# Context scores in the banks of transposes and outputs, and weight parts of four output projection tiles in the normalised input's memory

## The chip, the core and the metric

The kernel runs on one NeuronCore of a Trainium2 chip. The core has TensorE (matmuls, written to eight PSUM banks), VectorE, ScalarE and GpSimd for elementwise work, and SyncE, which here only issues transfers. Each engine works through its own list of instructions in order, and semaphores hold an instruction until its inputs are there and its output memory is free. The metric is the time of one execution on the device in microseconds (us); less is better.

## What is computed

One step of a two-layer backbone on 640 tokens of width 1024: 128 context tokens and 512 latent tokens. Each layer normalises its input, projects it to the inputs of three mixers (differential attention, a state-space mixer, neighbourhood attention), merges their outputs through sigmoid gates and adds an output projection. What matters here:

```python
def _diff_attention(q, k, v, lam):          # 4 heads, two score maps (m) per head
    p = _softmax32(jnp.einsum('bqhmd,bkhmd->bhmqk', qb, k) * scale)
    p = p[:, :, 0] - lam * p[:, :, 1]
    return jnp.einsum('bhqk,bkhe->bqhe', p.astype(v.dtype), v)
...
# context tokens read the 128 context keys; latent tokens read 512 latent keys and 256 cached ones
...
    merged = (ma * ((ya * jax.nn.silu(ga)) @ w_br_a) + mb * (yb @ w_br_b)
              + mc * ((yc * jax.nn.silu(gc)) @ w_br_c))
    return x + gate * (merged @ w_out)
```

## The kernel before

Activations lie with channels on the partitions, so a projection is a chain of matmuls over eight blocks of 128 channels (`feat`, L175: 128 outputs by 320 tokens at a time, a "half" of the 640). Every product of two float32 factors is done as three matmuls of a high and a low part (`hi`, `lo`). A weight tile is loaded to `raw` (two buffers), ScalarE copies its high part (L150) and VectorE subtracts it for the low part (L151); the pools `whi` and `wlo` have three buffers each. `mm` has three PSUM banks.

PSUM in the differential attention: three banks `mm`, one tile `s` of three banks (pool `ps`, one buffer) for scores, one bank `t` for transposes and one bank `o` for outputs (pool `pp`, one buffer each).

`diff_attn` does one head: the context first, then four query tiles of 128 tokens. For a query tile TensorE writes both score maps to `s` (L547, L551), VectorE takes the row maxima of both (L510) and scales them (L511), ScalarE makes both exponentials with their sums (L513; the tiles `e0` and `e1` have one buffer each), VectorE combines the maps (L514, L515, L517). Then two sets of three transposes go through the one bank `t` (L558), each copied by ScalarE (`ph`, L560) and subtracted by VectorE (`pl`, L561), and after two query tiles 18 matmuls with the values (L566) and a copy (L568). The context is the same with 128 keys: scores L526, transpose L529, copy L531, product L533. `diff_norm` squares the output (L576), sums columns on TensorE (L201) and makes rows of factors (L593); `diff_out` applies them (L604). Other work is written around it and fills TensorE meanwhile: the value projections of the next heads (L187, split by ScalarE L422 and VectorE L423), projections for the next mixer, and merge gates (`logit`: tanh evacuation L1061).

`out_proj` runs once per half (tokens 0 to 319, then 320 to 639): eight tiles m of 128 output channels, each with its own weight tile; VectorE adds gate times result to x (L1110). Half 0 comes right after the last merges. The normalised input `h` (eight high and eight low tiles of 128 x 640) is not read any more by then.

The order of each engine's instructions is not that of the program text: an automatic scheduler orders the whole program by its own estimate of when each operation can start, within what buffers allow. A small edit can so move instructions far from it.

Of the kernel before, what the change touches and what calls it, by code (L numbers as in the profile page):

```python
# [36 lines left out]
LC = ((0,), (1,), (2, 3), (4, 5, 6, 7))  # L37
MA = ((0,), (), (1,), (2, 3))

M_ID, M_TF, M_TB, M_LE, M_GE, M_ONE = range(6)  # L40
# [82 lines left out]


class Net:
    def __init__(self, nc, tc, a, o, dump=None):
# [15 lines left out]
    def weights(self, src, k, n):  # L142

        nc = self.nc
        view = lambda t: t[:, 0:k * n].rearrange("p (k n) -> p k n", k=k)
        raw = view(self.wraw.tile([128, 1056], F32, tag="raw", name="raw"))
        self.dma(raw, src)
        hi = view(self.whi.tile([128, 1056], F32R, tag="hi", name="hi"))
        lo = view(self.wlo.tile([128, 1056], F32R, tag="lo", name="lo"))
        nc.scalar.activation(hi, raw, AF.Copy)  # L150
        nc.vector.tensor_tensor(out=lo, in0=raw, in1=hi, op=ALU.subtract)  # L151
        return hi, lo

    def w_part(self, l, m, part):
# [341 lines left out]
    def diff_attn(self, l, h, v, kq, nlam, p, cp, ps, pp, after_ctx):  # L496
# [9 lines left out]
        def soft(s, n, t):  # L506

            st = p.tile([128, 4], F32, tag="st", name="st", bufs=3)
            e = [p.tile([128, 768], F32, tag=f"e{m}", name="e", bufs=1)[:, 0:n] for m in range(2)]
            nc.vector.tensor_reduce(out=st[:, 0:2], in_=s, axis=AX.X, op=ALU.max)  # L510
            nc.vector.tensor_scalar(out=st[:, 0:2], in0=st[:, 0:2], scalar1=-0.125, scalar2=None, op0=ALU.mult)  # L511
            for m in range(2):
                nc.scalar.activation(e[m], s[:, m], AF.Exp, bias=st[:, m:m + 1], scale=0.125, accum_out=zz[:, t, m:m + 1])  # L513
            nc.vector.reciprocal(st[:, 2:3], zz[:, t, 1:2])  # L514
# [5 lines left out]
        def bank3():  # L520
            return ps.tile([128, 1536], F32, tag="s", name="s")


        s = bank3().rearrange("p (b n) -> p b n", b=3)[:, 0:2, 0:128]
        for m in range(2):
            nc.tensor.matmul(s[:, m, :], lhsT=qx[half[m], :], rhs=kx[half[m], :], start=True, stop=True)  # L526
        e = soft(s, 128, 0)
# [575 lines left out]

    def out_proj(self, l, mg, x, gate, half):
        nc, a = self.nc, self.a
        for m in range(8):
            def evac(_, ps):
# [4 lines left out]

            self.feat(self.weights(a["w_out"][l, m], 8, 128), mg, evac, halves=(half,))

# [174 lines left out]
```

## Time and profile before

| | |
|---|---|
| runs | 1611.29 us median of 3 (1610.94 to 1612.96) |
| profiled execution | 1611.84 us, span 1610.1 us |
| granted TensorE clock, mean | 0.997 |
| TensorE busy | 1583.1 us, 98% of the span |
| VectorE / ScalarE / GpSimd busy | 66% / 48% / 10% |

Times in a trace count from the start of the span; the 1.7 us between the span and the execution's time lie around it. TensorE is nearly always busy, so its idle stretches are what another order can win or lose. A wait is read as: idle time of the engine before an instruction, and who released it.

### The profile page before, as it was taken

How to read it: one execution, taken by the hardware profiler on the slowest of the kernel's cores; microseconds unless marked ns; L12 is line 12 of the kernel's file. 1: busy time of each engine (PE TensorE's matmuls, PEld its weight loads, DVE VectorE, ACT ScalarE, POOL GpSimd, SP SyncE). 2: the span in 40 equal slices, each digit the busy share in tenths (PEclk: the TensorE clock that was granted, in tenths of full speed). 3: DMA queues.
4: the chain of work that ended last, by engine and by line, in shares of the span. 5: the costliest groups of instructions: out<-in, count | busy, mean ns of one | idle time of the engine just before them, and what ended most of it. 6: DMA issues, size and time to landing. Idle time of an engine off the chain costs nothing.

```text
span 1610.1 us, 29172 instructions
## 1 busy us (share of the span) xinstructions
PE 1583.1 (98%) x11371; PEld 1508.3 (94%) x11371; DVE 1064.1 (66%) x2299; ACT 774.1 (48%) x1790; POOL 155.8 (10%) x182
## 2 busy tenths in 40 slices
PE   8999999999999999999999999999999999999998
PEld 5999899999999999999989989999999999999998
DVE  5865688667556566756677667676575575577565
ACT  4535654344445555443455466334444555454342
POOL 2003421011000000000000252101010000000000
PEclk9999999999999999999999999999999999999999
DMA  9663225321225343436543222452122543344543
GB/s 340 210 244 112 89 93 160 125 75 56 85 88 162 127 127 110 151 115 245 185 164 133 85 75 82 139 174 74 60 89 78 161 127 89 112 133 155 207 168 131
DMA packets 81673, 214.63 MB, mean 133 GB/s; under 512 B 9728, under 2 KB 25664, under 8 KB 80512
## 3 DMA queue, kind: packets, MB, share of 16 engines
q1 hardware_dynamic: 80624, 211.46, 40.1%
q8 instruction: 90, 1.47, 0.4%
q0 software_dynamic: 480, 0.88, 0.2%
q10 hardware_dynamic: 432, 0.43, 0.1%
q14 instruction: 47, 0.39, 0.1%
HBM read 170.27 MB, written 34.08 MB: 127 GB/s over the span
## 4 chain that ended last, share of the span: by engine, by line
PE 89%; DVE 4%; DMA 3%; ACT 1%; issue 1%; POOL 1%; SPq 0%; DVEq 0%; ACTq 0%; POOLq 0%
PE mm L175 61%; PE mm L187 7%; PE s L1001 2%; PE o L1025 2%; PE o L566 2%; PE t L1017 2%; PE ex L175 2%; PE s L551 1%; PE g L813 1%; PE t L558 1%; DMA aw<-in_w_ada 1%; PE y L826 1%; PE y L268 1%; PE s L547 1%; DMA qd<-qr 1%
## 5 line engine op out<-in xcount | busy, mean ns | idle before, releaser
L175 PE MATMUL mm<-hl,hi 128*128 128x320 f32 x1856 | 577.8, 311 | 0.8 <-DVE hl L383 0.8
L175 PE MATMUL mm<-hh,hi 128*128 128x320 f32 x1856 | 574.5, 310 | 3.3 <-ACT hh L382 2.8
L175 PE MATMUL mm<-hh,lo 128*128 128x320 f32 x1856 | 573.5, 309 | 0.2 <-DVE lo L151 0.2
L175 PEld LDWEIGHTS mm<-hh,hi 128*128 128x128 f32 x1856 | 348.4, 188 | 11.6 <-ACT hh L382 4.1
L175 PEld LDWEIGHTS mm<-hh,lo 128*128 128x128 f32 x1856 | 348.9, 188 | 7.3 <-issue 4.7
L175 PEld LDWEIGHTS mm<-hl,hi 128*128 128x128 f32 x1856 | 348.5, 188 | 6.3 <-issue 2.6
L151 DVE TENSOR_TENSOR lo<-raw,hi 128x1024 fp32r<-128x1024 f32 (+2 forms) x194 | 235.6, 1215 | 93.7 <-ACT hi L150 90.7
L150 ACT ACTIVATE hi<-raw 128x1024 fp32r<-128x1024 f32 (+2 forms) x194 | 200.1, 1032 | 177.5 <-PE mm L175 116.5
L175 PE MATMUL mm<-yh,hi 128*128 128x320 f32 x320 | 98.8, 311 | 1.1 <-DVE th L1080 0.7
L175 PE MATMUL mm<-yl,hi 128*128 128x320 f32 x320 | 99.0, 310 | 0.0
L175 PE MATMUL mm<-yh,lo 128*128 128x320 f32 x320 | 99.0, 310 | 0.0
L187 PE MATMUL mm<-hi,hh 128*128 128x264 f32 (+1 forms) x320 | 90.5, 284 | 1.8 <-DVE vl L423 1.7
L187 PE MATMUL mm<-lo,hh 128*128 128x264 f32 (+1 forms) x320 | 91.0, 285 | 0.0
L187 PE MATMUL mm<-hi,hl 128*128 128x264 f32 (+1 forms) x320 | 90.6, 284 | 0.0
L560 ACT ACTIVATE ph<-t 128x384 fp32r<-128x384 f32 x64 | 31.4, 490 | 113.9 <-PE t L558 113.9
L175 PE MATMUL mm<-mgh,hi 128*128 128x320 f32 x256 | 78.7, 311 | 1.7 <-ACT hi L150 1.7
L175 PE MATMUL mm<-mgl,hi 128*128 128x320 f32 x256 | 79.9, 312 | 0.0
L175 PE MATMUL mm<-mgh,lo 128*128 128x320 f32 x256 | 78.7, 309 | 1.0 <-DVE lo L151 1.0
L510 DVE TENSOR_REDUCE st<-s 128x2 f32<-128x1536 f32 (+1 forms) x40 | 59.5, 1487 | 25.6 <-PE s L551 24.0
L1018 ACT ACTIVATE ph<-t 128x512 fp32r<-128x512 f32 x64 | 38.3, 598 | 68.4 <-PE t L1017 68.0
L513 ACT ACTIVATE e<-s,st 128x768 f32<-128x768 f32 (+1 forms) x80 | 62.8, 795 | 15.1 <-DVE st L511 15.1
L561 DVE TENSOR_TENSOR pl<-t,ph 128x384 fp32r<-128x384 f32 x64 | 35.5, 554 | 49.9 <-ACT ph L560 49.4
(351 smaller groups left out, 3052.8 us busy)
## 6 DMA issues: line engine op xcount, KB each, us to landing
raw<-in_w_feat SPq DMA_DIRECT2D x110, 512.0 KB, 3.6
aw<-in_w_ada SPq DMA_DIRECT2D x8, 2048.0 KB, 8.2
raw<-in_w_out SPq DMA_DIRECT2D x32, 512.0 KB, 3.6
thd<-th SPq DMA_DIRECT2D x48, 320.0 KB, 2.2
th<-thd SPq DMA_DIRECT2D x48, 320.0 KB, 3.7
raw<-in_w_br SPq DMA_DIRECT2D x24, 512.0 KB, 3.5
accd<-th SPq DMA_DIRECT2D x32, 320.0 KB, 2.8
ac<-accd SPq DMA_DIRECT2D x32, 320.0 KB, 4.3
```

Source lines behind the costliest of these rows:

```text
L150: nc.scalar.activation(hi, raw, AF.Copy)
L151: nc.vector.tensor_tensor(out=lo, in0=raw, in1=hi, op=ALU.subtract)
L175: nc.tensor.matmul(ps, lhsT=s, rhs=r, start=(k == 0 and n == 0), stop=(k == K - 1 and n == 2))
L187: nc.tensor.matmul(ps, lhsT=s, rhs=r, start=(k == 0 and q == 0), stop=(k == 7 and q == 2))
L510: nc.vector.tensor_reduce(out=st[:, 0:2], in_=s, axis=AX.X, op=ALU.max)
L513: nc.scalar.activation(e[m], s[:, m], AF.Exp, bias=st[:, m:m + 1], scale=0.125, accum_out=zz[:, t, m:m + 1])
L561: nc.vector.tensor_tensor(out=pl[dst], in0=pt[:, 0:3, :], in1=ph[dst], op=ALU.subtract)
L566: nc.tensor.matmul(ov[:, 0:256], lhsT=x[:, kt, sv], rhs=q[:, kt, :], start=(kt == 0 and n == 0), stop=(kt == 5 and n == 2))
L1001: nc.tensor.matmul(s[:, c0:c0 + n], lhsT=q[:, i * 128:(i + 1) * 128], rhs=ks[j][:, k0:k0 + n], start=(x == 0), stop=(x == 1))
L1017: nc.tensor.transpose(pt[:, t, :], e[:, t * 128:(t + 1) * 128], self.ident)
L1018: nc.scalar.activation(ph[:, i], pt, AF.Copy)
L1025: nc.tensor.matmul(out, lhsT=lw, rhs=sel(q), start=(first and x == 0), stop=(last and x == 1))
```

## The change

The context's two score maps (128 x 128 each) go into the one-bank tiles `t` and `o` instead of the three-bank tile `s`; the maxima are then taken by two reductions instead of one. In half 0 of the output projection the weight parts of m = 0, 2, 4 and 5 are written into tiles of `h` (four tiles of 640 columns for each m: columns 0 to 639 and 640 to 1023 of high and low part), so that for these a split is two instructions on ScalarE and two on VectorE, and `whi` and `wlo` serve only m = 1, 3, 6 and 7. The loads and the matmuls stay. In all ScalarE has 1569 instructions instead of 1561, VectorE 2285 instead of 2269, TensorE 10801 as before.

```diff
+SPARE = (0, 2, 4, 5)
+
+class Rows:
+    def __init__(self, tiles):
+        self.parts = [t.rearrange("p (k n) -> p k n", k=5) for t in tiles]
+
+    def __getitem__(self, at):
+        p, k, c = at
+        return self.parts[k // 5][p, k % 5, c]
...
+    def weights_in(self, src, tiles):
+        nc = self.nc
+        raw = self.wraw.tile([128, 1056], F32, tag="raw", name="raw")[:, 0:1024]
+        self.dma(raw.rearrange("p (k n) -> p k n", k=8), src)
+        for i, c in enumerate((slice(0, 640), slice(640, 1024))):
+            hi, lo = (tiles[2 * j + i][:, 0:c.stop - c.start] for j in range(2))
+            nc.scalar.activation(hi, raw[:, c], AF.Copy)
+            nc.vector.tensor_tensor(out=lo, in0=raw[:, c], in1=hi, op=ALU.subtract)
+        return Rows(tiles[0:2]), Rows(tiles[2:4])
...
-            nc.vector.tensor_reduce(out=st[:, 0:2], in_=s, axis=AX.X, op=ALU.max)
+            if isinstance(s, list):
+                for m in range(2):
+                    nc.vector.tensor_reduce(out=st[:, m:m + 1], in_=s[m], axis=AX.X, op=ALU.max)
+            else:
+                nc.vector.tensor_reduce(out=st[:, 0:2], in_=s, axis=AX.X, op=ALU.max)
+                s = [s[:, m] for m in range(2)]
...
-                nc.scalar.activation(e[m], s[:, m], AF.Exp, bias=st[:, m:m + 1], scale=0.125, accum_out=zz[:, t, m:m + 1])
+                nc.scalar.activation(e[m], s[m], AF.Exp, bias=st[:, m:m + 1], scale=0.125, accum_out=zz[:, t, m:m + 1])
...
-        s = bank3().rearrange("p (b n) -> p b n", b=3)[:, 0:2, 0:128]
+        s = [pp.tile([128, 512], F32, tag=t, name=t)[:, 0:128] for t in ("t", "o")]
         for m in range(2):
-            nc.tensor.matmul(s[:, m, :], lhsT=qx[half[m], :], rhs=kx[half[m], :], start=True, stop=True)
+            nc.tensor.matmul(s[m], lhsT=qx[half[m], :], rhs=kx[half[m], :], start=True, stop=True)
...
     def out_proj(self, l, mg, x, gate, half):
         nc, a = self.nc, self.a
+        free = [t for k in range(8) for t in self.h[k]]
+        spare = {m: free[4 * i:4 * i + 4] for i, m in enumerate(SPARE)} if half == 0 else {}
...
-            self.feat(self.weights(a["w_out"][l, m], 8, 128), mg, evac, halves=(half,))
+            src = a["w_out"][l, m]
+            w = self.weights_in(src, spare[m]) if m in spare else self.weights(src, 8, 128)
+            self.feat(w, mg, evac, halves=(half,))
```

The scheduler moves much with it. Three places follow; numbers behind a name tell one buffer's use from the next.

**First pair, TensorE at the end of head 1, layer 0.** `s_4008` is the last query tile's score set before the change, `mm_4419` a value projection. Before:

```order
L551 MATMUL s_4008<-ks_3344,ql_3348 128x512
L175 MATMUL mm_4373<-hh6_93,lo_4344 128x320
L175 MATMUL mm_4373<-hh7_95,hi_4343 128x320
L558 MATMUL t_3996<-masks_135,e_3987 128x128 x3
L175 MATMUL mm_4373<-hl7_96,hi_4343 128x320
L175 MATMUL mm_4373<-hh7_95,lo_4344 128x320
L187 MATMUL mm_4419<-hi_4409,hh0_81 128x256
L187 MATMUL mm_4419<-lo_4410,hh0_81 128x256
L187 MATMUL mm_4419<-hi_4409,hl0_82 128x256
L187 MATMUL mm_4419<-hi_4409,hh1_83 128x256
```

115 rows lie there between the last row of `s_4008` and the next score set; most are value projections (L187). In the changed order the same score set is `s_4012`, the value projection is `mm_4504` (line L212 now), scores are L577 and L581, transposes L588, and `s_4617` is the first query tile of head 2:

```order
L581 MATMUL s_4012<-ks_3346,qh_3348 128x512
L581 MATMUL s_4012<-ks_3346,ql_3350 128x512
L212 MATMUL mm_4504<-hi_4419,hl6_94 128x256
L212 MATMUL mm_4504<-hi_4419,hh7_95 128x256
L212 MATMUL mm_4504<-lo_4420,hh7_95 128x256
L212 MATMUL mm_4504<-hi_4419,hl7_96 128x256
L588 MATMUL t_4000<-masks_135,e_3991 128x128 x3
L588 MATMUL t_4006<-masks_135,e_3991 128x128 x3
L577 MATMUL s_4617<-ks_4063,qh_4065 128x256
```

Between the two score sets four matmuls and two sets of transposes are left, and the context scores of head 2 come later. On VectorE, after the change, at the same place (L539 the reduction, L591 the low part of the probabilities, L547 the combination):

```order
L547 SCALAR_TENSOR_TENSOR e_3991<-e_3992,st_3990,e_3991 128x768
L539 TENSOR_REDUCE st_4021<-s_4012 128x2
L591 TENSOR_TENSOR pl_3980<-t_4000,ph_3979 128x3x128
L541 TENSOR_SCALAR st_4021<-st_4021 128x2
L591 TENSOR_TENSOR pl_3980<-t_4006,ph_3979 128x3x128
L610 RECIPROCAL rz_4566<-zz_3863 128x5
```

The low part that frees the transposes' bank stands behind the reduction of the next score set. Layer 1 has the same order here.

**Second pair, ScalarE at the output projection, layer 0.** `hi_9010` and `hi_9043` are the high parts of m = 3 and 4, before:

```order
L150 ACTIVATE hi_8977<-raw_8975 128x1024
L1090 ACTIVATE mgh6_8579<-th_8817 128x640
L1090 ACTIVATE mgh7_8581<-th_8852 128x640
L150 ACTIVATE hi_9010<-raw_9008 128x1024
L150 ACTIVATE hi_9043<-raw_9041 128x1024
L331 ACTIVATE acc_9181<-x0_8893 128x320
L334 ACTIVATE sq_9183<-x1_8894 128x320
```

Both stand behind the evacuations of the last merges (L1090). After the change, L164 is a split into the pools (`hi_9018` is m = 3), L175 one into `h` (two rows each for m = 2, 4 and 5), L1120 an evacuation of the last merges:

```order
L1120 ACTIVATE mgh4_8583<-th_8749 128x640
L175 ACTIVATE hh2_85<-raw_8983 128x640
L175 ACTIVATE hl2_86<-raw_8983 128x384
L164 ACTIVATE hi_9018<-raw_9016 128x1024
L1120 ACTIVATE mgh5_8585<-th_8784 128x640
L175 ACTIVATE hh4_89<-raw_9049 128x640
L175 ACTIVATE hl4_90<-raw_9049 128x384
L1120 ACTIVATE mgh6_8587<-th_8825 128x640
L1120 ACTIVATE mgh7_8589<-th_8860 128x640
L175 ACTIVATE hh6_93<-raw_9082 128x640
```

The splits of m = 3, 4 and 5 now stand among the last merges.

**Third pair, ScalarE at the context of head 3, layer 0.** L531 is the copy of the context's transpose and L513 the exponentials of a query tile, before:

```order
L1061 ACTIVATE th_5342<-mm_5349 128x320
L568 ACTIVATE of_4578<-o_4757 128x256
L531 ACTIVATE px_5099<-t_5097 128x128
L576 ACTIVATE sq_5058<-of_4578 128x640
L513 ACTIVATE e_5125,zz_5083<-s_5115,st_5124 128x768
L513 ACTIVATE e_5126,zz_5083<-s_5115,st_5124 128x768
L150 ACTIVATE hi_5560<-raw_5558 128x1024
L1061 ACTIVATE th_5342<-mm_5375 128x320
```

The squares and a context evacuation lie around the copy. After (L561 is the copy, L543 the exponentials, `s_5123` the first query tile):

```order
L922 ACTIVATE early_5565<-mm_5572 128x128
L909 ACTIVATE early_5565<-mm_5572 128x7x24
L561 ACTIVATE px_5107<-t_5105 128x128
L543 ACTIVATE e_5133,zz_5089<-s_5123,st_5132 128x768
L543 ACTIVATE e_5134,zz_5089<-s_5123,st_5132 128x768
L910 ACTIVATE early_5565<-mm_5572 128x24
```

On TensorE the transposes, the context's product and the next score set now stand together, with nothing between:

```order
L200 MATMUL mm_5572<-hh7_95,lo_5569 128x320
L559 MATMUL t_5105<-masks_135,e_5095 128x128
L563 MATMUL o_5109<-px_5107,vx_4406 128x128
L577 MATMUL s_5154<-ks_4783,qh_4785 128x256
L577 MATMUL s_5154<-ks_4783,ql_4787 128x256
```

What stood between them before, merge projections, comes after the scores. Layer 1 has the same order.

## Rows read from the trace of the kernel before

**Rows 1.** The page, part 1: busy time, share of the span, instructions of each engine.

```profile
PE 1583.1 (98%) x11371; PEld 1508.3 (94%) x11371; DVE 1064.1 (66%) x2299; ACT 774.1 (48%) x1790; POOL 155.8 (10%) x182
```

**Rows 2.** TensorE's waits: who it waited for, us in total, times, longest.

```profile
PE s L547 <- ACT e L513: 1.7, 3, 1.1
PE mm L187 <- DVE vl L423: 1.7, 1, 1.7
PE mm L175 <- ACT hi L150: 1.7, 4, 0.5
PE mm L175 <- DVE lo L151: 1.2, 3, 0.5
PE t L558 <- DVE pl L561: 0.5, 2, 0.3
PE mm L175 <- ACT th L1061: 0.4, 1, 0.4
```

**Rows 3.** TensorE's timeline, end of head 1, layer 0: start, duration, tiles [idle before].

```profile
372.53 0.38 PE L547 MATMUL s<-ks,qh 128*128 128x256 f32 x1 [0.21 <-ACT e L513]
374.03 0.28 PE L566 MATMUL o<-pl,vh 128*128 128x256 f32 x1
374.99 0.27 PE L529 MATMUL t<-masks,e 128*128 128x128 f32 x1
376.98 0.39 PE L187 MATMUL mm<-hi,hh 128*128 128x256 f32 x1 [1.72 <-DVE vl L423]
```

**Rows 4.** ScalarE's timeline, same place.

```profile
369.28 0.49 ACT L560 ACTIVATE ph<-t 128x384 fp32r<-128x384 f32 x1 [4.56 <-PE t L558]
375.07 0.63 ACT L413 ACTIVATE vh<-vr 128x512 fp32r<-128x512 f32 x1 [2.60 <-PE o L566]
376.82 0.77 ACT L576 ACTIVATE sq<-of 128x640 f32<-128x640 f32 x1
377.45 0.93 ACT L513 ACTIVATE e<-s,st 128x768 f32<-128x768 f32 x1
378.32 0.94 ACT L513 ACTIVATE e<-s,st 128x768 f32<-128x768 f32 x1
379.20 1.10 ACT L150 ACTIVATE hi<-raw 128x1024 fp32r<-128x1024 f32 x1
```

**Rows 5.** VectorE's timeline, same place.

```profile
369.81 0.56 DVE L561 TENSOR_TENSOR pl<-t,ph 128x384 fp32r<-128x384 f32 x1 [3.52 <-ACT ph L560]
374.23 1.76 DVE L510 TENSOR_REDUCE st<-s 128x2 f32<-128x1536 f32 x1 [0.87 <-PE s L551]
379.38 0.17 DVE L514 RECIPROCAL st<-zz 128x1 f32<-128x1 f32 x1 [1.73 <-ACT e L513]
379.96 1.02 DVE L517 SCALAR_TENSOR_TENSOR e<-e,st 128x768 f32<-128x768 f32 x1
```

**Rows 6.** Groups by line: the tanh evacuation; count, then busy us and mean ns.

```profile
L1061 ACT ACTIVATE th<-mm 128x320 f32<-128x320 f32 x96 | 41.0, 427 | 42.6 <-PE mm L175 37.3 <-issue 4.1 <-ACT rh L812 1.0
```

**Rows 7.** TensorE's timeline, start of the output projection, layer 0.

```profile
766.13 0.42 PE L175 MATMUL mm<-mgh,hi 128*128 128x320 f32 x1 [0.46 <-ACT hi L150]
768.15 0.41 PE L175 MATMUL mm<-mgh,lo 128*128 128x320 f32 x1 [0.51 <-DVE lo L151]
```

**Rows 8.** ScalarE's and VectorE's timelines, same place.

```profile
765.02 2.01 ACT L150 ACTIVATE hi<-raw 128x1024 fp32r<-128x1024 f32 x2 [3.66 <-PE mm L175]
765.12 1.84 DVE L1110 SCALAR_TENSOR_TENSOR x<-mm,gate,x 128x128 f32<-128x128 f32 x6 [2.90 <-PE mm L175]
766.88 2.35 DVE L151 TENSOR_TENSOR lo<-raw,hi 128x1024 fp32r<-128x1024 f32 x2
```

**Rows 9.** Windows: length, busy us by engine, granted clock, DMA share, GB/s.

```profile
765.00:768.00 3.00, 1.79 (x9) 1.00 (x7) 2.88 (x7) 2.98 (x5) 0.00 (x0) 1.00 0.38 129
769.00:772.00 3.00, 3.00 (x13) 3.00 (x13) 1.12 (x3) 0.65 (x1) 0.00 (x0) 0.50 0.86 273
828.00:833.00 5.00, 2.60 (x12) 1.59 (x12) 3.87 (x10) 2.44 (x6) 0.13 (x1) 1.00 0.00 0
```

## The prediction

> **What bounds the kernel now.** I read the page's busy times first: TensorE is busy for 98% of the span [rows 1], so the time is TensorE's work plus its gaps. The list of its waits says who ends them [rows 2]. For both layers together they hold 2.9 us before the first output projection (weight splits, L150 and L151) and 4.3 us in the differential attention (1.7 on the exponentials, 1.7 on the value parts, 0.5 on a low part of the probabilities, 0.4 on a tanh evacuation). Last I read the timelines of the two places that the change touches: the end of head 1 [rows 3 to 5] and the start of the output projection [rows 7, 8]. There is little to win and 1,583 us of tightly packed matmuls to disturb, so the question is what the new order does to the packing.
>
> **The output projection.** Now the tiles m = 0, 1 and 2 fill the three weight buffers and the three banks, and the splits of m = 3 and 4 start only when the first of these come free: on ScalarE 2.01 us for two from 765.02, on VectorE 2.35 us for two behind six residual updates [rows 8]. TensorE idles 0.46, then twice more, the last time 0.51 [rows 7]; both layers together 1.7 + 1.2 = 2.9 us [rows 2]. In the change m = 0, 2, 4 and 5 need no buffer of the three, so m = 3 is split while the last merges still run (second order pair). What is left is the bank: tile 3 waits for the update of x0, two of six instructions that take 1.84 together from 765.12, so about 0.67 and done near 765.8, against running matmuls that end near 765.7. I keep 0.2 per layer. Gain 2.9 - 0.4 = 2.5 us. The four spare tiles cost one instruction more on ScalarE and on VectorE each; they lie beside merges of several us, and I price them at nothing (their cover gone, a split pair costs 1.10 + 1.2 once). The weights' loads leave SyncE in the same order, sooner, since a raw buffer is free as soon as its split is done; the loads of x are queued behind them there and are wanted only at the first update.
>
> Behind this stall the granted clock stood at 0.50 for 3 us in layer 0 [rows 9], the lower of the two levels (1.2 GHz), while TensorE had been busy 1.79 of the 3 us before it. 3 us at half speed cost 1.5 us, which go too. Without the clock the part gains 2.5, with it 4.0.
>
> **The context scores.** By itself this removes one hold on the three-bank tile per head: the context's scores no longer wait for the last tile's exponentials, and the next query tile no longer waits for the context's (0.21 at 372.53 [rows 3]). One more reduction per head (under 0.3) is hidden. But the scheduler now puts the scores of the next head's first query tile ahead of the context's work, and uses up the value projections (L187) earlier, which lay beneath the softmax before.
>
> To price this I lay the instructions of a stretch end to end in the new order, each at its row's duration, starting when its engine is free and its inputs are there. On the order before, this gives gaps of 0.38 and 1.88 where the rows show 0.21 and 1.72 [rows 3], and 0.57 and 0.76 where they show 0.46 and 0.51 [rows 7]. It is long by 0.1 to 0.25, so I take 0.15 off every gap.
>
> *Group B, end of head 1 (first order pair).* Time 0 is the start of the scores s_4012. Eight matmuls take 1.50, from 372.53 to 374.03 [rows 3]; with the drain VectorE's reduction runs from 1.6 to 3.35 (1.76 [rows 5]). TensorE has four value matmuls left (0.12 each, as the eight from 374.03 to 374.99 [rows 3]) and three transposes, and stands at 2.25. The next transposes need the same one bank, which the low part (L561, 0.56 [rows 5]) frees; that subtraction stands behind the reduction on VectorE, so the bank is free at 3.9: **gap 1.64**. Then ScalarE copies the high part (0.49 [rows 4]), and only behind it come both exponentials of s_4012: the second starts 0.87 after the first and its sum is read 1.06 after its own start, at 378.32 and 379.38 [rows 4, 5]. TensorE is done with those transposes at 4.3, and the next scores (s_4617) come right behind, at 6.85: **gap 2.51**. The combination of the two maps takes 1.60 from the reciprocal [rows 5], nearly the length of those scores. The first product waits for a copy (0.49 plus starting up, **0.74**), the second transposes for the low part (0.56, **0.38**), the later products for theirs (**0.27**). Then the column sums stand first on TensorE. They need the squares, and ScalarE reaches those only after a value split, three value copies and the copy of the output: before, from the start of that split (375.07) to the end of the squares (377.59) passed 2.52 with the same instructions and one more between them [rows 4]. **2.49**, and 0.19 for a value part. Sum 8.2; less 0.15 for each of seven gaps, 7.2 per layer. Before, 0.21 + 1.72 were lost here in layer 0, less in layer 1; they are in the 4.3.
>
> *Group D, context of head 3 (third order pair).* The product waits for a copy (L531) that ScalarE does behind two others: 0.76. The next scores wait for two exponentials that stand behind that copy, 0.87 + 1.06 less what ran meanwhile: 1.56. Before, a merge filled this place. With a 1.05 wait for the norm's rows ahead of it and a 1.0 wait for an evacuation behind a split after it: 4.37, less 0.6 is 3.8.
>
> *Group A, first half of head 1.* Two of three matmul banks hold gates not yet evacuated, so each merge waits for the tanh of the one before (0.43 [rows 6]), with short transposes alone as cover: 0.56. Where a split (1.10 [rows 4]) stands ahead of it: 1.35, and 0.97 with four short matmuls beneath. 2.88, less 0.45 is 2.4.
>
> *Group C, heads 2 to 3.* The exponentials stand behind a copy whose transposes come four matmuls before the next scores: 0.49 + 0.87 + 1.06 less 0.35 is 2.07. With five plain evacuation waits (0.15 to 0.67) it is 3.8, less 0.9 is 2.9.
>
> *Group E, start of the neighbourhood attention.* Six short waits per layer, each for an evacuation or a sum one to three instructions back; no row has them. Each lies between nothing and a split plus an evacuation (1.10 + 0.43). I take 0.6, nearer to the plain evacuation: 3.6.
>
> Per layer 7.2 + 3.8 + 2.4 + 2.9 + 3.6 = 19.9, for both 39.8, in place of 4.3. Each gap also costs a start: the first matmul after one takes 0.38 instead of 0.28, as at 372.53 and 374.03 [rows 3]. Some 44 gaps in place of 10: 3.4.
>
> **The clock in group B.** TensorE works there for less than half of 15 us. The nearest rows disagree: after 1.79 busy us in 3 the clock fell, in the stretch from 828 to 833 with 2.60 busy in 5 it stayed at 1.00 [rows 9]. Bounds: nothing, or 1.5 at each place. I take 1.5 for group B in both layers, 3.0, and nothing elsewhere.
>
> The Trainium skill ("TensorE: Matmul & The Clock Gate", section "A second HAM failure mode: psum-queue depth-cycling") tells of a kernel that cycles through banks, idles briefly between groups of matmuls and so sees its clock go down and up again. By that rule all five groups of each layer would lose speed; by the row at 828 none would. That is the second rival.
>
> **Sum.** 39.8 - 4.3 + 3.4 - 2.5 - 1.5 + 3.0 = +37.9. The profiled execution took 1611.84, 0.55 above the median of the runs, so 1611.29 + 37.9 = **1649.2 us**.
>
> **Rivals.**
> 1. *The short waits are covered.* Of all gaps only those stay where TensorE has nothing else to issue: group B, the 1.9 of C, and 2.0 of D; 11.1 per layer. For it: the laying-out is long on short gaps, and where it gives 0.2 the rows before often show none. Against it: it has no bias on gaps above 1 us. 22.2 - 4.3 + 0.8 - 2.5 - 1.5 = +14.7, 1626 us, or 1629 with the clock falling in B.
> 2. *The clock falls in every group,* ten times 1.5 in place of twice: +12, 1661 us. For it: the fall at 769. Against it: the stretch at 828, emptier and without a fall [rows 9].
> 3. *No new waits; the other side.* The context leaves the three-bank tile, transposes and evacuations of different banks overlap, and the 4.3 vanish with the 4.0 of the projection: 1603 us. It decides at group B: between s_4012 and s_4617 TensorE would need 4 us of other work, some 34 value matmuls at 0.12. The order has four and six transposes.
> The Trainium skill ("Perfetto Trace Analysis", section "Optimizing Tensor Performance", Matmuls) wants independent groups of matmuls rotated through different banks, so that evacuation overlaps the next group. By it the context part gains. The order speaks against it here: what is late is VectorE's reduction, not a bank.
> 4. *The projection gains nothing,* since the m = 3 split is late after all or another wait takes its place: +4.0, 1653 us. Inside the range either way.
>
> **Chances.** Forecast 0.57 (its own range 1637 to 1658), rival 1 0.16, rival 2 0.17, rival 3 0.04, rival 4 0.06. The range 1630 to 1663 leaves out rival 3 and most of rival 1. A change below 0.2% (3.2 us) is about what a measurement cannot tell from none. Faster needs rival 3, 0.04; same needs half of the gaps of rival 1 gone as well, 0.02; slower 0.94.
>
> **What the profile after would show.** Right: TensorE's busy share falls to some 96%; the scores' wait for the exponentials is the longest in its list, some 11 us for both layers in gaps of 1.4 to 2.5; the column sums wait over 2 us twice for the squares; the output projection waits for no split, and the clock stays at 1.00 there; granted clock at 0.50 near the end of head 1. Wrong: the scores' wait under 5 us (the exponentials finish under other work), or column sums without a wait; and if the time is far above 1663, a transfer that feeds a split is late, which I gave nothing.

## The result and the profile after

The change makes the kernel slower: 1668.39 us median of 4 runs (1666.34 to 1669.72) against 1611.12 us (1610.21 to 1612.96, 4 runs) of the kernel before on the same chip, a ratio of 1.0349, 95% interval 1.0336 to 1.0362. The profiled execution took 1669.72 us, its span 1667.6. The prediction was 1649.2 with a range up to 1663, so the direction was right and the size too small by 19 us.

The page after, the span and part 1, beside [rows 1]:

```profile
span 1667.6 us, 29191 instructions
PE 1611.2 (97%) x11371; PEld 1527.7 (92%) x11371; DVE 1069.3 (64%) x2315; ACT 776.3 (47%) x1798; POOL 157.5 (9%) x182
```

The span grew by 57.5 us. TensorE's idle time (span less busy) grew from 27.0 to 56.4, by 29.4, and its busy time by 28.1 with the same 11371 instructions. So only half of the loss is waiting; the other half is matmuls that took longer.

The waits of TensorE after that bear on the change, beside [rows 2] (who it waited for, us in total, times, longest). Scores are now L577 and L581, exponentials L543, transposes L588, `pl` L591, context scores L556, squares L606, column sums L226, rows L623, the projection `feat` L200, its update of x L1143:

```profile
PE s L577 <- ACT e L543: 11.0, 6, 2.3
PE mm L200 <- ACT th L1091: 4.2, 8, 1.2
PE o L226 <- ACT sq L606: 3.9, 2, 2.0
PE mm L200 <- ACT vf L910: 3.6, 2, 1.8
PE t L1047 <- DVE st L1042: 3.2, 2, 1.6
PE t L588 <- DVE pl L591: 3.2, 3, 1.5
PE o L556 <- DVE rows L623: 1.9, 2, 1.0
PE mm L200 <- DVE x L1143: 0.6, 2, 0.3
```

The scores' wait for exponentials grew from 1.7 to 11.0, the transposes' for the low part from 0.5 to 3.2, the projections' for a tanh evacuation from 0.4 to 4.2. New are the column sums' wait for the squares and a wait of the context's scores for the normalisation rows of the previous head, which hold bank `o`. The splits of the output projection are gone from the list; 0.3 per layer on the update of x is left.

TensorE's timeline after, layer 0, the longest waits and one shorter (idle before in brackets): the end of head 1, then head 2, the context of head 3, and the start of the neighbourhood attention. Layer 1 has nearly the same rows.

```profile
374.70 0.55 PE L588 MATMUL t<-masks,e 128*128 128x128 f32 x3 [1.51 <-DVE pl L591]
377.59 0.39 PE L577 MATMUL s<-ks,qh 128*128 128x256 f32 x1 [2.35 <-ACT e L543]
380.72 0.58 PE L596 MATMUL o<-ph,vh 128*128 128x256 f32 x1 [0.58 <-ACT ph L590]
388.21 1.54 PE L226 MATMUL o<-masks,sq 128*128 128x1 f32 x10 [1.98 <-ACT sq L606]
449.71 0.39 PE L577 MATMUL s<-ks,qh 128*128 128x256 f32 x1 [1.90 <-ACT e L543]
473.14 0.49 PE L556 MATMUL o<-kx,qx 64*128 64x128 f32 x2 [0.97 <-DVE rows L623]
479.80 0.38 PE L577 MATMUL s<-ks,qh 128*128 128x256 f32 x1 [1.27 <-ACT e L543]
524.22 0.42 PE L200 MATMUL mm<-hh,hi 128*128 128x320 f32 x1 [1.79 <-ACT vf L910]
549.04 0.67 PE L1047 MATMUL t<-masks,e 128*128 128x128 f32 x4 [1.62 <-DVE st L1042]
```

The clock at these places, in windows of the kernel after (length, busy time of PE, PEld, DVE, ACT and POOL, granted clock, DMA share, GB/s):

```profile
378.00:386.00 8.00, 7.41 (x33) 6.04 (x32) 2.18 (x4) 1.31 (x3) 0.00 (x0) 0.57 0.00 0
389.00:393.00 4.00, 4.00 (x23) 4.00 (x22) 1.80 (x10) 0.45 (x1) 1.17 (x1) 0.57 0.00 0
450.00:454.00 4.00, 4.00 (x17) 3.72 (x17) 2.31 (x3) 0.93 (x2) 0.00 (x0) 0.57 0.39 110
525.00:529.00 4.00, 4.00 (x19) 4.00 (x18) 2.85 (x7) 3.32 (x11) 0.00 (x0) 0.58 1.02 306
549.00:553.00 4.00, 3.96 (x17) 3.59 (x18) 3.24 (x11) 2.08 (x6) 0.00 (x0) 0.57 0.00 0
768.00:773.00 5.00, 5.00 (x36) 5.00 (x35) 4.35 (x8) 2.54 (x3) 0.34 (x6) 1.00 0.97 333
```

In the same windows of the kernel before, the first five stood at 1.00 and the last at 0.66. A stretch at the lower level (1.2 GHz) costs at most TensorE's busy time in it times one less the clock: 7.41 x 0.43 = 3.2 us in the first row, 4.00 x 0.43 = 1.7 in each of the next four. Idle time in such a stretch is counted as idle already and costs nothing more. Added up over the whole span in windows of 1 us (the stretch behind the last matmul left out), the clock cost 24.2 us after and 3.2 before. Counted by its length alone, each stretch has 1.7 us of lost clock or a small multiple of it. In such units of length there are 15 after and 2 before; what a unit costs is 1.7 us or a little less.

So the 57.5 us are 29.4 of idle time, 21.0 of clock, and a remainder of 7.1 in which TensorE counts as busy. A part of the remainder lies at the gaps: a last matmul before a gap shows its full 0.27, where those in a run start 0.12 apart, and the first one after it takes 0.38 in place of 0.28 [rows 3]. The trace after has 54 gaps of 0.15 us and more, the one before 32; 22 more at 0.25 each are an estimate of 5.5 us.

### The profile page after: what moved, and what is told of

It reads as the page before. It is cut to its first block, busy times and chain, and to the rows that moved or that the text cites. A ratio compares the mean times of both kernels' runs of the same rounds, so it can differ in the third digit from the quotient of the medians.

```text
span 1667.6 us, 29191 instructions
## 1 busy us (share of the span) xinstructions
PE 1611.2 (97%) x11371; PEld 1527.7 (92%) x11371; DVE 1069.3 (64%) x2315; ACT 776.3 (47%) x1798; POOL 157.5 (9%) x182
## 4 chain that ended last, share of the span: by engine, by line
PE 89%; DVE 3%; DMA 3%; ACT 3%; issue 1%; SPq 0%; POOL 0%; DVEq 0%; ACTq 0%; POOLq 0%
PE mm L200 61%; PE mm L212 7%; PE s L1031 2%; PE o L596 2%; PE s L581 2%; PE t L1047 2%; PE o L1055 2%; DMA raw<-in_w_out 1%; PE t L588 1%; PE g L843 1%; PE y L856 1%; PE s L577 1%; PE y L293 1%; ACT hi L164 1%; DMA x<-in_x 1%
## 5 line engine op out<-in xcount | busy, mean ns | idle before, releaser
L200 PE MATMUL mm<-hh,hi 128*128 128x320 f32 x1856 | 578.5, 312 | 11.9 <-ACT th L1091 4.2
L200 PE MATMUL mm<-hl,hi 128*128 128x320 f32 x1856 | 579.6, 312 | 0.6 <-DVE hl L408 0.6
L200 PE MATMUL mm<-hh,lo 128*128 128x320 f32 x1856 | 576.1, 310 | 0.0
L200 PEld LDWEIGHTS mm<-hh,hi 128*128 128x128 f32 x1856 | 350.8, 189 | 22.7 <-ACT th L1091 6.7
L200 PEld LDWEIGHTS mm<-hh,lo 128*128 128x128 f32 x1856 | 351.1, 189 | 7.4 <-issue 4.7
L200 PEld LDWEIGHTS mm<-hl,hi 128*128 128x128 f32 x1856 | 350.8, 189 | 5.7 <-issue 2.7
L164 ACT ACTIVATE hi<-raw 128x1024 fp32r<-128x1024 f32 (+2 forms) x186 | 191.8, 1031 | 201.5 <-PE mm L200 149.9
L165 DVE TENSOR_TENSOR lo<-raw,hi 128x1024 fp32r<-128x1024 f32 (+2 forms) x186 | 224.5, 1207 | 86.1 <-ACT hi L164 83.0
L200 PE MATMUL mm<-yl,hi 128*128 128x320 f32 x320 | 100.2, 314 | 0.2 <-DVE yl L1082 0.2
L200 PE MATMUL mm<-yh,hi 128*128 128x320 f32 x320 | 99.3, 315 | 0.6 <-DVE st L541 0.6
L200 PE MATMUL mm<-yh,lo 128*128 128x320 f32 x320 | 99.2, 310 | 0.0
L212 PE MATMUL mm<-hi,hh 128*128 128x264 f32 (+1 forms) x320 | 92.6, 291 | 1.0 <-ACT th L1091 1.0
L212 PE MATMUL mm<-lo,hh 128*128 128x264 f32 (+1 forms) x320 | 92.5, 290 | 0.0
L212 PE MATMUL mm<-hi,hl 128*128 128x264 f32 (+1 forms) x320 | 91.9, 288 | 0.0
L591 DVE TENSOR_TENSOR pl<-t,ph 128x384 fp32r<-128x384 f32 x64 | 35.4, 553 | 70.0 <-ACT ph L590 69.8
L539 DVE TENSOR_REDUCE st<-s 128x2 f32<-128x1536 f32 x32 | 56.1, 1753 | 26.7 <-PE s L581 26.5
L212 PEld LDWEIGHTS mm<-hi,hh 128*128 128x128 f32 x320 | 62.0, 194 | 2.3 <-ACT th L1091 1.5
L1035 DVE CUSTOM_DVE_ANT_0 e<-s,bias 128x256 f32<-128x256 f32 x64 | 27.0, 422 | 57.0 <-PE t L1047 40.2
L212 PEld LDWEIGHTS mm<-lo,hh 128*128 128x128 f32 x320 | 62.0, 194 | 1.1 <-issue 0.8
L200 PEld LDWEIGHTS mm<-yl,hi 128*128 128x128 f32 x320 | 60.6, 190 | 2.1 <-DVE yl L428 0.8
```

The source lines that it names most:

```text
L200: nc.tensor.matmul(ps, lhsT=s, rhs=r, start=(k == 0 and n == 0), stop=(k == K - 1 and n == 2))
L212: nc.tensor.matmul(ps, lhsT=s, rhs=r, start=(k == 0 and q == 0), stop=(k == 7 and q == 2))
L591: nc.vector.tensor_tensor(out=pl[dst], in0=pt[:, 0:3, :], in1=ph[dst], op=ALU.subtract)
```

## The experiments

Two theories were to be told apart. **Theory O:** the context's second map needs bank `o`, which the previous head's outputs and normalisation hold until its rows (L623) are made; the two exponential tiles `e0` and `e1` tie the next query tile's exponentials to the context's; so the chain from head to head gets longer, the fill-in work runs out, and the gaps bring the clock down. **Rival R**, in the prediction's words: the scheduler "uses up the value projections (L187) earlier". "Clock" in this table is the sum as above, with the number of units in brackets; idle is the span less TensorE's busy time, all from the profiled execution of each. The median is that of the runs; each ratio is to runs of the kernel before on the same chip, whose medians were 1611.1 to 1613.0.

| kernel | median us | ratio to before [95%] | idle | clock (units) |
|---|---|---|---|---|
| before | 1611.12 | | 27.0 | 3.2 (2) |
| after | 1668.39 | 1.0349 [1.0336, 1.0362] | 56.4 | 24.2 (15) |
| projection part only | 1610.29 | 0.9990 [0.9981, 0.9999] | 24.6 | 6.6 (4) |
| context part only | 1672.44 | 1.0376 [1.0354, 1.0399] | 58.0 | 19.6 (12) |
| maps in `t` and `mm` | 1644.03 | 1.0191 [1.0174, 1.0208] | 38.5 | 20.4 (13) |
| maps in `mm` and `o` | 1693.02 | 1.0500 [1.0484, 1.0517] | 81.0 | 19.5 (18) |
| own exponentials | 1658.77 | 1.0286 [1.0267, 1.0305] | 49.7 | 20.9 (13) |
| late value projections | 1669.32 | 1.0355 [1.0336, 1.0373] | 56.1 | 26.9 (17) |
| normalisation in `mm` | 1666.49 | 1.0325 [1.0308, 1.0343] | 48.5 | 36.6 (25) |
| both links cut | 1620.53 | 1.0048 [1.0034, 1.0063] | 30.6 | 8.3 (5) |
| projection part, own exponentials | 1607.91 | 0.9971 [0.9959, 0.9983] | 22.0 | 6.4 (4) |

The clock column is one execution of each kernel, and the number of falls is not fixed for a kernel. The mean granted clock of the 32 executions of the kernel before that ran beside the experiments lay between 0.993 and 0.997, with a median of 0.995; the profiled one had 0.997. That of the kernel after lay between 0.983 and 0.986, and that of the context part alone between 0.978 and 0.987, with times from 1667.5 at the highest clock to 1675.3 at the lowest. A thousandth is 1.6 us of clock, about one unit. So 15 units against 2 are a difference of the kernels; two to four units between two traces can be one of the executions.

### Each part alone

The projection part alone is the kernel after with the maximum and the context's score lines put back; one of these lines:

```diff
-        s = [pp.tile([128, 512], F32, tag=t, name=t)[:, 0:128] for t in ("t", "o")]
+        s = bank3().rearrange("p (b n) -> p b n", b=3)[:, 0:2, 0:128]
```

> Only the weight parts of the output projection in the normalised input's memory; the context scores stay in the three-bank tile. All theories: 1611.1 - 2.5 for the waits on splits - 1.7 for the half-clock stretch behind them (0.19 + 3 x 0.5 in the trace of before) = 1607 us, granted clock at 1.00 between 765 and 773, the differential attention as before. If rival 4 of the prediction were right: 1611.

The context part alone has the projection's call put back:

```diff
-            src = a["w_out"][l, m]
-            w = self.weights_in(src, spare[m]) if m in spare else self.weights(src, 8, 128)
-            self.feat(w, mg, evac, halves=(half,))
+            self.feat(self.weights(a["w_out"][l, m], 8, 128), mg, evac, halves=(half,))
```

> Only the context scores in the banks of transposes and outputs. All of the loss should be here: 1668.4 + 2.5 for the waits on splits, and up to 1.7 more if the clock falls behind them: 1671 to 1673 us.

All the loss is the context's: 1672.44 with it alone, 1610.29 with the other part alone. The projection part does at its place what the prediction said. TensorE's timeline there holds one wait in place of three, of which [rows 7] show two:

```profile
765.33 0.38 PE L200 MATMUL mm<-mgh,hi 128*128 128x320 f32 x1 [0.28 <-DVE x L1138]
```

Its windows there and at the normalisation at the start of layer 1:

```profile
768.00:773.00 5.00, 5.00 (x37) 5.00 (x36) 3.40 (x6) 1.42 (x2) 0.00 (x0) 1.00 0.89 259
827.00:835.00 8.00, 7.30 (x29) 7.04 (x30) 8.00 (x21) 4.29 (x10) 0.00 (x0) 0.57 0.33 94
```

Half speed is gone at 768 and stands at 827 instead, for twice the cost (3.2 in place of 1.7), in the stretch in which the kernel before kept 1.00 [rows 9]. A further 3.4 lie at 11 to 19. So this execution has 2.4 us less of idle time and 3.4 more of clock than the profiled one of the kernel before. The runs do not show that the part costs clock: the median granted clock is 0.995 in its 11 executions and in the 15 of the kernel before beside them. They show a ratio of 0.9990, 1.6 us less: near the idle time won, short of the 4 us expected, and below the 0.2% that the prediction takes as what can be told from none.

### Which bank

The context's maps stand in `t` and one of the three `mm` banks, or in an `mm` bank and `o`:

```diff
-        s = [pp.tile([128, 512], F32, tag=t, name=t)[:, 0:128] for t in ("t", "o")]
+        s = [b[:, 0:128] for b in (pp.tile([128, 512], F32, tag="t", name="t"), self.bank())]
```

> As the changed kernel, but the context's second score map goes into a matmul bank (mm) instead of the output bank o. Theory O: the bank o is the cause, because the norm of the head before holds it from its column sums to its rows, so that the context's scores come late, and through the single exponential tiles the first query tile's exponentials too. Then over half of the added waits go, about 20 of 37 us, and about half of the half-clock stretches with them (10 of 19 us): 1637 us, the wait of the scores for exponentials under 8 us in total. Theory R (rival): the loss is the scheduler's new order as such, with any one-bank tiles: 1655 to 1672, as the changed kernel.

> As the changed kernel, but the first map in a matmul bank instead of the transposes' bank t, the second in o as in the change. Theory O: as slow as the changed kernel or slower, since o stays and one matmul bank less is there for merges; laid end to end with the durations of the rows its waits are 15 us more: 1680 to 1690 us. Theory R: the same as t_mm within 5 us. If the bank t were the cause, this one would be the fast one of the pair, near 1637.

Without `o` 24 us come back; with `o` and without `t` 25 more are lost, 49 apart where rival R gave at most 5. Of the two banks `o` is the one that costs more; it is not the whole loss, since with `t` and `mm` 33 us of the 57 are left. Some of the waits of the kernel with `mm` and `o` (1693, 3 above what theory O gave):

```profile
PE s L577 <- ACT e L543: 15.2, 10, 2.3
PE mm L200 <- ACT e L543: 12.3, 4, 3.2
PE o L556 <- DVE rows L623: 9.6, 4, 4.0
```

The context's wait for `o` grew from 1.9 to 9.6 us, and the projections now wait too (12.3), for the `mm` bank that holds the context's other map until its exponential is done. With `t` and `mm` the context's scores wait on rows no more (its product, which goes to `o`, does, 2.0 us in two waits); the first two rows are these:

```profile
PE s L577 <- ACT e L543: 6.2, 4, 2.8
PE o L226 <- ACT sq L606: 5.3, 4, 1.9
```

That kernel missed its expected 1637 by 7 us: idle time fell to 38.5, but 13 units of clock are left.

### Which link, and the rival

Two kernels follow. In the first the context's exponentials go into the memory of its own keys and queries, dead by then, and leave `e0` and `e1` to the query tiles; in the second the value projections of heads 2 and 3 are held back behind the last scores of head 1 (`self.mark` is the last score matmul written so far; the line that sets it is left out here):

```diff
-            e = [p.tile([128, 768], F32, tag=f"e{m}", name="e", bufs=1)[:, 0:n] for m in range(2)]
+            e = [qx, kx] if n == 128 else [p.tile([128, 768], F32, tag=f"e{m}", name="e", bufs=1) for m in range(2)]
```

> As the changed kernel, but the context's exponentials go into the tiles kx and qx, dead by then, instead of the two single tiles that the query tiles use. Theory O has two links: the context comes late (bank o), and the first query tile's exponentials wait for the context's through the single tiles. This cuts the second link only. So part of the loss goes: laid end to end with the rows' durations, about 9 us of waits less, and two or three half-clock stretches of 1.7: 1654 to 1660 us. Theory R (the order as such): no change, 1665 to 1672.

```diff
-                                    v = self.diff_v(l, 1, vp)
+                                    with tc.issue_after(self.mark.ins):
+                                        v = self.diff_v(l, 1, vp)
```

> As the changed kernel, but the value projections of heads 2 and 3 may be issued only behind the last score matmul of head 1, so that they fill the place at the end of head 1 (group B of the prediction). Theory R, fillers used at the wrong place: the 5 us of waits on the bank of transposes and on the exponentials there go, with two half-clock stretches per layer: 1648 to 1655 us. Theory O, the chain of each head is longer and other work is short: they go there and open earlier in head 1 in the same size: 1663 to 1673 us.

The second link is worth 9.6 us (1668.39 less 1658.77). The scores' wait fell from 11.0 to this:

```profile
PE s L577 <- ACT e L543: 5.9, 3, 2.3
```

Held back value projections do not change the time (1669.32, its interval overlaps that of the kernel after). The gap only moves to a tile earlier, and the lower clock with it; TensorE's timeline of that kernel:

```profile
356.56 0.38 PE L577 MATMUL s<-ks,qh 128*128 128x256 f32 x1 [2.65 <-ACT e L543]
```

Its windows there and where the kernel after had lost:

```profile
357.00:368.00 11.00, 9.46 (x39) 8.09 (x38) 6.78 (x12) 4.24 (x10) 0.00 (x0) 0.53 0.10 37
378.00:386.00 8.00, 7.23 (x54) 6.36 (x52) 1.74 (x4) 2.14 (x6) 0.00 (x0) 1.00 0.00 0
```

378 to 386, at 0.57 in the kernel after, is at 1.00 here, and 357 to 368 is at 0.53. Rival R, which gave 1648 to 1655, falls: wherever this work stood, another place was bare.

### The normalisation out of bank o, and both links cut

```diff
-        ov = pp.tile([128, 512], F32, tag="o", name="o")
+        ov = self.bank()
```

This line is in `diff_norm`; it frees `o` sooner.

> The changed kernel, with one edit: the column sums, rows and product of the head's normalisation stand in an mm bank, not in bank o, so that the context's second map no longer has to wait for the previous head's rows before it may be written. The exponential tiles e0 and e1 stay shared. Theory O (the longer chain from head to head through bank o and the exponentials makes the gaps, and the gaps in a row bring the half-clock stretches): the first link goes and the second stays, so part of the loss comes back, 1652 to 1663 us, and the wait of the context's scores (L556) on rows (L623) is gone. Rival R (the context work stands in the wrong place because value projections are used up early, whatever the banks): as the changed kernel, 1665 to 1671. Rival C (the transposes' bank t is what costs, not o): also 1665 to 1671.

A miss for theory O: 1666.49, inside what rivals R and C said (C: the bank `t` is what costs), with an interval that overlaps that of the kernel after. The wait on rows is gone and idle time fell by 7.9 us, but TensorE's busy time grew by 5.4, with ten units of clock more. Of TensorE's waits in that kernel the longest, and the one of the context's scores:

```profile
PE t L588 <- DVE e L547: 9.6, 2, 4.8
PE o L556 <- ACT of L598: 1.5, 2, 0.7
```

The first of the waits on `e` in TensorE's timeline:

```profile
485.27 0.87 PE L588 MATMUL t<-masks,e 128*128 128x128 f32 x3 [4.79 <-DVE e L547]
```

The window around and behind it:

```profile
482.00:500.00 18.00, 12.89 (x52) 11.94 (x53) 6.10 (x18) 5.11 (x12) 1.28 (x1) 0.53 0.44 161
```

Two things stand against a plain reading. Bank `o` is still held by the previous head's outputs (L598 is their copy), so the link was loosened and not cut. And a new wait came, once in each layer: ScalarE's timeline shows the exponentials of a query tile behind a split and a tanh evacuation that themselves wait for TensorE.

```profile
476.76 0.43 ACT L1091 ACTIVATE th<-mm 128x320 f32<-128x320 f32 x1
480.04 1.06 ACT L164 ACTIVATE hi<-raw 128x1024 fp32r<-128x1024 f32 x1 [2.85 <-PE mm L200]
481.01 0.42 ACT L1091 ACTIVATE th<-mm 128x320 f32<-128x320 f32 x1
481.32 0.48 ACT L590 ACTIVATE ph<-t 128x384 fp32r<-128x384 f32 x1
481.69 0.90 ACT L543 ACTIVATE e<-s,st 128x768 f32<-128x768 f32 x1
```

The scores were ready and their scaled maxima too (VectorE ended them at 477.8), and ScalarE idled 2.85 us in front of a split that the scheduler had put first. Around each of the two gaps of 4.79 the clock was low for five units; by TensorE's busy time there that cost 6.3 us each. The run by itself decides nothing between the theories.

The next kernel takes neither `t` nor `o` for the context and has its own exponentials as well:

```diff
-        s = [pp.tile([128, 512], F32, tag=t, name=t)[:, 0:128] for t in ("t", "o")]
+        s = [b[:, 0:128] for b in (self.bank(), self.bank())]
```

> The changed kernel with both links cut: the context's two maps stand in two mm banks, neither in t nor in o, and the context's exponentials in the memory of its key and query tiles, not in e0 and e1. Theory O: the chain from head to head is as short as in the kernel before, gaps and half-clock stretches of the attention go, and the time is that of the kernel before within half a per cent, 1608 to 1618 us. Rival R (the early use of the value projections, or the context's order in itself, costs): 1640 to 1668 us, with half-clock stretches left at the end of head 1.

1620.53: 48 of the 57 us are back, 2.5 above the upper end of what theory O gave and 20 below the rival's lower end. The end of head 1 has no wait on TensorE between 370 and 392, and the windows of the three worst places read:

```profile
378.00:395.00 17.00, 15.77 (x120) 15.20 (x120) 9.29 (x27) 7.59 (x18) 1.20 (x2) 1.00 0.19 66
448.00:456.00 8.00, 7.80 (x56) 7.49 (x55) 4.77 (x11) 4.25 (x9) 1.17 (x1) 1.00 0.30 109
546.00:554.00 8.00, 8.00 (x58) 7.68 (x57) 4.46 (x15) 3.79 (x11) 0.00 (x0) 1.00 0.46 164
```

All stand at 1.00. The 8.4 us that its span has over the one before are 3.6 of idle time and some 5 of clock, elsewhere: single gaps of 1.9 us at 255 and 351 with one unit each, and one each at 839 and 1037. The two cuts together give more than one after the other: 9.6 for the exponentials, 24 for the bank, 48 for both. Here `t` is free as well, and no run parts that from the two cuts; so what holding `t` costs is not shown.

### A version that beats both

The projection part with the context's maps back in the three-bank tile, and the context's exponentials in its keys and queries (the diff of own exponentials above).

> The output projection's part of the change, context scores in the three-bank tile as before, and the context's exponentials in kx and qx. Theory O: the second link is cut where the first never was; the waits of the first query tile's scores and of the value parts in head 1 shrink, 2 to 3 us less than spare_only: 1607 to 1609 us, the fastest so far. Theory R makes no statement; if the tiles of the exponentials were no link, 1610.

1607.91, 0.29% below the kernel before on the same chip. Its page:

```profile
span 1605.5 us, 29174 instructions
PE 1583.5 (99%) x11371; PEld 1510.8 (94%) x11371; DVE 1069.4 (67%) x2307; ACT 773.3 (48%) x1798; POOL 155.6 (10%) x182
```

Idle time falls to 22.0, 5.0 less than before, and 0.29% is 4.7 us. Its trace has four units of clock in place of two, no more than executions of one kernel differ by.

### What a single gap does to the clock

This kernel computes nothing of the reference (its outputs are zeros): 64 blocks of 64 equal matmuls, and between two blocks a gap that one or two instructions on ScalarE set.

> No part of the computation: 64 blocks of 64 matmuls (128 x 128 by 320 columns, 9.4 us each), and between them TensorE waits for one or two ScalarE instructions that write the next block's input; all results are zeros. Eight lengths of gap (about 0.5, 1.0, 1.15, 1.3, 1.45, 1.55, 2.05 and 2.55 us), eight times each, mixed. It measures the disputed price, what a lone gap brings: the prediction took 1.5 us for the place with many gaps and nothing for lone ones. By the trace of the changed kernel a lone gap of 1.8 to 1.9 us was followed by a half-clock stretch of 1.7 us in two of four places, one of 1.2 us in none of two. If length decides alone, each length gives 0 of 8 or 8 of 8; if something else has a share, the middle lengths give a part of 8, rising with the length.

| gap, us | 0.6 | 1.1 | 1.3 | 1.5 | 1.6 | 1.7 | 1.8 | 2.1 | 2.5 |
|---|---|---|---|---|---|---|---|---|---|
| falls / gaps | 0/8 | 0/8 | 0/8 | 0/7 | 0/7 | 0/8 | 0/1 | 2/8 | 4/8 |

A fall, at a gap of 2.53 that ends at 133.72, in its window:

```profile
133.00:137.00 4.00, 3.28 (x12) 3.28 (x13) 0.00 (x0) 0.67 (x1) 0.00 (x0) 0.58 0.02 4
```

Each is one unit again (4.00 x 0.42 = 1.7 us by length). Between long busy blocks a lone gap of up to 1.8 us brought none in 47. In the kernel after, gaps of that size between other gaps did: 1.90 at 449 and 1.79 at 524 in layer 0, while their counterparts of the same length in layer 1 (1260 and 1335) did not. Whether a given gap brings a fall is so not told by its length; what decides it stays open.

## Why the prediction was right and wrong

**The gaps: right.** The five groups were predicted at 19.9 us a layer and measure 18.4 in layer 0: 1.7 for 2.4 (A), 6.4 for 7.2 (B), 2.8 for 2.9 (C), 3.4 for 3.8 (D), 4.1 for 3.6 (E). In B the largest two came at 1.51 and 2.35, where the laying-out gave 1.64 and 2.51 before 0.15 was taken off each, and the column sums at 1.98 for 2.49, just under the 2 us named as a sign. The scores' wait of "some 11 us" was 11.0. Over the span, idle time was predicted to grow by 39.8 - 4.3 - 2.5 = 33.0 and grew by 29.4. Group E, priced between far bounds with no row of its own, came out right in sum by luck: three gaps stand where six were counted.

**The projection: right at its place.** No wait on a split, 0.28 per layer for the update of x (0.2 predicted), clock 1.00 from 768 to 773.

**The clock: the step that failed.** "I take 1.5 for group B in both layers, 3.0, and nothing elsewhere" had a right mechanism at one place and a wrong size everywhere. Group B lost three units, 4.9 us, in each layer and not 1.5; C lost one unit more, D one and E three over both layers, and A none. Sum over the groups 18.1 (11 units) for 3.0. To that come 3.0 at the program's start and 1.6 at 860, in the normalisation at the start of layer 1, which no step of the prediction touched, less 1.7 at 768: 21.0 in all where the sum had +1.5. Rival 2, that the clock falls in every group, named this, at 15 in place of 18.1, and gave 1661; its ten falls of one size were not what came. The row on which it was discounted, 828 to 833 with no fall [rows 9], was no guide. It is that same normalisation, with three gaps in a row; TensorE's timeline of the kernel before:

```profile
828.90 0.78 PE L362 MATMUL rb<-d,root 128*128 128x320 f32 x2 [0.63 <-DVE d L361]
830.91 0.71 PE L175 MATMUL mm<-hh,hi 128*128 128x320 f32 x3 [1.23 <-ACT hh L382]
832.16 0.41 PE L175 MATMUL mm<-hl,hi 128*128 128x320 f32 x1 [0.54 <-DVE hl L383]
```

The same work in TensorE's timeline of the kernel after:

```profile
857.80 0.78 PE L387 MATMUL rb<-d,root 128*128 128x320 f32 x2 [0.60 <-DVE d L386]
859.81 0.94 PE L200 MATMUL mm<-hh,hi 128*128 128x320 f32 x3 [1.24 <-ACT hh L407]
861.05 0.63 PE L200 MATMUL mm<-hl,hi 128*128 128x320 f32 x1 [0.31 <-DVE hl L408]
```

The window of the kernel after there:

```profile
860.00:864.00 4.00, 3.69 (x15) 3.30 (x15) 4.00 (x10) 2.36 (x6) 0.00 (x0) 0.57 0.00 0
```

The same work waits nearly the same time, and once the clock stays and once it falls. With nearly these gaps it fell in eight of the eleven traces of the full kernel, and stayed in that of the kernel before, with the normalisation in `mm` and with the maps in `mm` and `o`. One place without a fall was read as a rule, and it was one draw. The Trainium skill ("TensorE: Matmul & The Clock Gate", section "A second HAM failure mode: psum-queue depth-cycling"), which the prediction weighed against that row, had the direction: brief idling between groups of matmuls makes the clock go down and up. The trace agrees, with 11 units in B to E, and shows too that not each such place falls.

With 18.1 for 3.0 the prediction's sum is 53.0, and 1664 us.

**The starts: too small.** 3.4 was predicted, for 34 more gaps at 0.10. The growth of busy time that the clock does not account for is 7.1, with 22 more gaps. The price left out what the last matmul before a gap shows (0.15 by [rows 3]); with it the estimate is 5.5, and where the last 1.6 lie is open.

By terms, measured less predicted: idle 29.4 - 33.0 = -3.6, clock 21.0 - 1.5 = +19.5, remainder for starts 7.1 - 3.4 = +3.7; sum +19.6, and 37.9 + 19.6 = 57.5. This is the one pair of traces; that of the kernel before stands at the high end of its granted clock (0.997), and by the median of its other executions (0.995) some 3 us of the 19.5 would be less.

**The reason for the order: right in part.** That less work stood between two score sets is what the order shows. Its cause is not that value projections were used early: held back, they cover the scores at the end of head 1 and bare another place. The longer chain through bank `o` and the exponential tiles is what the runs with other banks support. That "what is late is VectorE's reduction, not a bank", said against rival 3, holds for the single gap at 374, and not for the change as a whole. How much of the 57 us belongs to each of the two links, and how much to `t`, is open: the run with both links cut freed `t` too, and the run in which only the normalisation left `o` brought a new wait of its own. The two units more at the program's start (one unit before and with the context part alone, three after) are no more than executions of one kernel differ by.

**The warning sign named for a time above 1663,** a late transfer behind a split, did not come: of the waits of TensorE after, none is on a weight split, and those on a transfer sum to 0.4 us.

## What to carry to other kernels

Before a tile is put into a bank that another long chain holds, look at what has to happen until that bank is free: here two context matmuls of together half a microsecond wait for a whole normalisation, and the next softmax waits behind them. On an engine that is busy for 98% of the time, price a new gap at its length plus what the clock takes behind it; here 29 us more of gaps came with 21 us more of clock. And lay out a longer stretch than the place edited: a gap that is filled by work from elsewhere has moved, not gone.

## What the runs showed of the hardware that was not expected

The stretches at the lower clock come in equal pieces: by length 1.70 us of lost clock, or two to five times that without a break (3.41 at 378, 8.53 around a gap of 4.79), in all kernels here. What is lost in time is less where TensorE idles in the stretch: 3.1 at 378, 6.3 around the gap of 4.79, and with the maps in `mm` and `o` 19.5 us in all for 18 units. A gap can so cost nearly as much behind it as in itself: one of 1.90 us cost 1.70 more, one of 4.79 with the two shorter ones after it (6.6 together) 6.3.

Nor are the pieces fixed by the kernel. At nearly the same gaps, those of the normalisation at the start of layer 1, the clock fell in eight traces of eleven, and executions of the kernel before differ by up to four thousandths of mean clock, some 6 us by length. A difference of a few units between single traces therefore says little about an edit; the mean granted clock of all runs has to be read beside it.
